# The gate product of a gated three-branch mixer by seven block products

## The chip, the cores and the metric

One core of a Trainium2 chip runs the whole kernel in one launch. The metric is device time in microseconds. TensorE (PE) multiplies matrices, VectorE (DVE) and ScalarE (ACT) do elementwise work, GpSimd (POOL) does some more of it, and SyncE (SP) issues the transfers between DRAM and the on-chip memory SBUF. PE writes its results to PSUM banks.

## What is computed

Two layers over 1024 tokens of width 1024 in float32. The change lies in the first, a mixer with three branches (a: spatial gating, b: dilated window attention, m: attention over a memory of 256 rows). Cut to what matters:

```python
h = rms_norm(x, norm_w)
proj = h @ w_in
a_u, a_v, a_z, b_q, b_k, b_v, b_z, m_q, m_z, g = jnp.split(proj, split_at, axis=-1)
...
y_m = y_m * jax.nn.silu(m_z)
gates = jax.nn.sigmoid(g.reshape(bn, s, 3, D_MODEL) + gate_b)
merged = (gates[:, :, 0] * (y_a @ proj_a)
          + gates[:, :, 1] * (y_b @ proj_b)
          + gates[:, :, 2] * (y_m @ proj_m))
x = x + merged @ w_out
```

The gate product g is 1024 tokens by 1024 by 3072 columns, and with 12 column-block pairs of 256 it is the largest product of the layer. The second layer (state-space mixer, two attentions, a final norm) is not touched by the change.

## The kernel before

Every float32 product is made of three products of a reduced-precision format: each operand is split into a high and a low part (hTh, hTl for the activations, whi, wlo for weights), and high x high, high x low and low x high are summed in PSUM. ACT makes the high part by a copy, DVE the low part by a subtraction (hilo, L266). In unitB (L372) the weights of 128 columns stand still and 512 tokens move past them: three matmuls of 128x512 for each of eight blocks k of 128 rows. In unitA the activations stand still.

The order of all instructions on each engine is fixed when the program is built. Every step is a small generator task with a priority. A planner (Sched, L81) keeps a clock for each engine from a table of costs (Eng, L145) and always continues the task that could start first. The numbers in its table are only used for the order. Pools limit how far it runs ahead: 20 tiles t4 of 128x1024 and 8 more for split weights, six t2 of 128x512, four PSUM banks "mm", three raw weight tiles, four slots "whl" for split weights (L189). Weights arrive in the order in which plan (L486) lists them: w_dma (L285) loads 512 KB into a raw tile wraw, and w_conv (L305) splits it into whi and wlo. All loads go through SP's queue.

dense (L631) sets the order of the first layer. dense_b runs the three groups of branch b in the order 1, 2, 0. For group 2 the columns (tokens) of hTh and hTl stand in residue order, four classes of tokens one after another. Ahead of group 0, reorder (L698) brings each k back to natural order, with a copy to a tile cv and a cast by DVE back into hTh[:, k] and hTl[:, k], 16 casts of 128x1024 in all, while PE does the product kv of the memory (dense_kv, L1334). dense_m (L1304) does branch m: for each head the product mz (48 matmuls), whose z_evac makes the factor silu(m_z), and then mq and the attention. dense_bz and dense_a follow, with preps in between, which prepares the second layer's constants (its transposes of ssm_c among them).

merge (L1230) then runs once for each branch in the order 0 (a), 2 (m), 1 (b). For each of the eight blocks db of 128 columns, it does the gate product for both token halves, tanh by ACT out of PSUM into tg, the projection (proj_a, proj_m or proj_b, 6, 4 or 2 blocks k) for both halves, and on DVE (tanh + 1) * projection from PSUM, added to the tile acc. The results of branches m and b wait in DRAM, and reload (L1209) brings them back and splits them. loads_1 (L1718) splits the sum for the output projection, out_proj_1 (L1754).

Of the kernel before, what the change touches and what calls it, by code (L numbers as in the profile page):

```python
# [180 lines left out]
class Kern:  # L181
# [103 lines left out]
    def w_dma(self):  # L285
        i = 0
        for w in self.wq:
            for g in w.grans:
# [16 lines left out]
    def w_conv(self):  # L305
        for w in self.wq:
            for g in w.grans:
# [11 lines left out]
                yield  # L319

# [51 lines left out]
    def unitB(self, w, csl, xh, xl, tsl, deps, cont, prio):  # L372
# [16 lines left out]
        self.s.spawn(cont(ps), prio, cont.__name__)  # L389

# [94 lines left out]

    def plan(self):  # L486
# [8 lines left out]
        for g in (1, 2, 0):  # L495
            if g == 0:
                for c in range(4):
                    add(("kv", c), I["m_w_kv"], 8, c * 256, 256)
            add(("bv", g), wi, 8, OFF_BV + g * 256, 256)
            add(("bk", g), wi, 8, OFF_BK + g * 256, 256)  # L500
            add(("bq", g), wi, 8, OFF_BQ + g * 256, 256)
        for hp in range(2):
            for s in range(2):
                add(("mz", 2 * hp + s), wi, 8, OFF_MZ + (2 * hp + s) * P, P)
            add(("mq", hp), wi, 8, OFF_MQ + hp * 256, 256)
# [125 lines left out]
    def dense(self, upto):  # L631
# [5 lines left out]
        if upto >= 2:  # L637
# [17 lines left out]
    def dense_b(self):  # L655
# [42 lines left out]
    def reorder(self, k, ev):  # L698

        for src in (self.hTh[:, k], self.hTl[:, k]):  # L700
# [225 lines left out]
    def z_evac(self, dst, ev):  # L926
        def cont(ps):
            self.A.activation(dst, ps, AF.Tanh, scale=0.5)
# [133 lines left out]
    def dense_a(self):  # L1062
# [44 lines left out]
        self.ya_ev = Ev()  # L1107
        left2 = [12]
        for j in range(6):
            um = {}  # L1110
# [28 lines left out]
            for th in range(2):  # L1139
                def cont(ps, th=th, um=um, yh=yh, yl=yl, um_ev=um_ev):  # L1140
# [12 lines left out]
                    self.rel("t2")  # L1153
                    left2[0] -= 1
                    if left2[0] == 0:
                        self.rel("t4", 2)
                        self.ya_ev.t = s.cur.t
# [34 lines left out]


# [36 lines left out]
    def merge(self, gi, yh, yl, deps):  # L1230

        s = self.s
        hh, hl = self.hk()
        first, last = self.acc is None, gi == 1
        if first:
            self.acc = {}
            self.acc_ev = [[Ev(), Ev()] for _ in range(8)]
        for db in range(8):
            wg, wp = self.w[("g", gi, db)], self.w[("p", gi, db)]
            if first and db % 2 == 0:  # L1240
                yield from self.acq("t4", 2)
                for th in range(2):
                    self.acc[db // 2, th] = self.t4(F32, "acc").rearrange("p (k t) -> p k t", k=2)
            tt = {}
            gev = [Ev(), Ev()]
            for th in range(2):
                def cont(ps, th=th, db=db, tt=tt, gev=gev):
                    if self.gb_ev.t is None:
                        yield self.gb_ev
                    yield from self.acq("t2")  # L1250
                    tt[th] = self.t2(F32, "tg")
                    self.A.activation(tt[th], ps, AF.Tanh, scale=0.5, bias=self.gb[:, gi * 8 + db:gi * 8 + db + 1])
                    self.rel("mm")
                    gev[th].t = s.cur.t
                yield from self.unitB(wg, slice(0, P), hh, hl, slice(th * 512, (th + 1) * 512), [], cont, 17)
            wg.done()
            for th in range(2):
                tsl = slice(th * 512, (th + 1) * 512)

                def cont(ps, th=th, db=db, tt=tt, gev=gev, tsl=tsl):  # L1260
                    yield gev[th]
                    a = self.acc[db // 2, th][:, db % 2, :]
                    t = tt[th]
                    if first:
                        self.V.scalar_tensor_tensor(a, t, 1.0, ps, op0=OP.add, op1=OP.mult)
                        self.rel("mm")
                    else:
                        self.V.scalar_tensor_tensor(t, t, 1.0, ps, op0=OP.add, op1=OP.mult)
                        self.rel("mm")
                        yield  # L1270
                        self.V.tensor_add(a, a, t)
                    self.rel("t2")
                    if last:
                        self.acc_ev[db][th].t = s.cur.t
                yield from self.unitB(wp, slice(0, P), lambda k: yh[k], lambda k: yl[k], tsl, deps, cont, 16)
            wp.done()
        self.rel("t4", 2 * len(yh))

# [25 lines left out]
    def dense_m(self):  # L1304
# [5 lines left out]
        self.ymT, self.mz_ev = {}, {}  # L1310
# [1515 lines left out]
```

## Time and profile before

| | us |
|---|---|
| median of 3 runs | 1783.63 (1781.91 to 1783.87) |
| profiled execution | 1782.18 |
| its span | 1780.5 |
| PE busy | 1728.5 |
| DVE busy | 1004.0 |
| ACT busy | 698.8 |
| POOL busy | 149.9 |

The span runs from the first to the last recorded instruction; the execution's own time is 1.7 us longer. Busy time is the time in which an engine has at least one instruction in flight. The matmuls of PE overlap, so the length of one matmul is more than the distance to the next. The rows name instructions as out<-in by the program's names, with partitions x elements; L239 is the helper that issues all products and L252 the transposes, L156 the helper for the other engines.

### The profile page before, as it was taken

Reading aid. Unit: us, or ns where it says so; the run is one execution under the profiler, and the core shown is the slowest. Engines: PE = TensorE matmul, PEld = TensorE weight load, DVE = VectorE, ACT = ScalarE, POOL = GpSimd, SP = SyncE. Lnnn points to the kernel's source line nnn. Section 1 sums busy time; section 2 is a strip of 40 time slices with the busy share of each in tenths; the row PEclk is TensorE's granted clock in tenths of the full one; section 3 lists DMA queues with packets and bytes.
Section 4 is the critical chain, followed back from the end, with each engine's and each line's share of the span. In section 5 each row is a group of like instructions: output and inputs, shape, how many; then the busy total and the mean of one; then the engine's idle time right before and its main releaser. Section 6 shows DMA issues by size and latency. Waiting matters only on the chain.

```text
span 1780.5 us, 26765 instructions
## 1 busy us (share of the span) xinstructions
PE 1728.5 (97%) x10215; PEld 1514.0 (85%) x10215; DVE 1004.0 (56%) x2621; ACT 698.8 (39%) x1602; POOL 149.9 (8%) x207
## 2 busy tenths in 40 slices
PE   7999979999999899999999999999999999999998
PEld 6999979998989787878888888888888788888787
DVE  6666774756655876631132243455268665655765
ACT  5464753544424122211121122366334534545632
POOL 1322322300100000000000000002000010100000
PEclk9999979999999999999999999999999999999999
DMA  6222131112033123631131122254231021112531
GB/s 223 81 67 70 49 110 36 37 51 69 28 117 84 56 78 102 206 114 54 36 101 42 52 96 66 83 179 133 66 92 47 31 72 48 37 36 83 190 127 75
DMA packets 158115, 147.80 MB, mean 83 GB/s; under 512 B 18284, under 2 KB 135582, under 8 KB 157988
## 3 DMA queue, kind: packets, MB, share of 16 engines
q1 hardware_dynamic: 157988, 146.09, 26.5%
q8 instruction: 81, 1.33, 0.3%
q14 instruction: 46, 0.38, 0.1%
HBM read 124.62 MB, written 23.80 MB: 83 GB/s over the span
## 4 chain that ended last, share of the span: by engine, by line
PE 83%; DVE 9%; ACT 3%; DMA 3%; issue 1%; POOL 1%; SPq 0%; POOLq 0%; ACTq 0%; DVEq 0%
PE psmm L239 69%; PE psx L239 9%; PE psx L252 4%; DVE dp L156 2%; ACT dp L156 1%; DVE wlo L156 1%; DVE scan L156 1%; DVE sp L156 1%; DMA sp<-in_ssm_log_step_dram 1%; DVE hTl L156 1%; DVE dst L156 0%; DMA xt<-in_x_dram 0%; SPq L256 0%; DVE St L156 0%; ACT whi L156 0%
## 5 line engine op out<-in xcount | busy, mean ns | idle before, releaser
L156 DVE TENSOR_TENSOR wlo<-wraw,whi 128x1024 fp32r<-128x1024 f32 (+3 forms) x161 | 183.0, 1139 | 212.2 <-ACT whi L156 199.4
L239 PE MATMUL psmm<-hTh,whi 128*128 128x512 f32 x672 | 266.3, 396 | 0.0
L239 PE MATMUL psmm<-whi,hTh 128*128 128x256 f32 x896 | 262.3, 293 | 1.4 <-ACT hTh L156 1.4
L239 PE MATMUL psmm<-hTl,whi 128*128 128x512 f32 x672 | 262.4, 390 | 0.0
L239 PE MATMUL psmm<-hTh,wlo 128*128 128x512 f32 x672 | 262.4, 390 | 0.0
L239 PE MATMUL psmm<-whi,hTl 128*128 128x256 f32 x896 | 254.3, 284 | 0.0
L239 PE MATMUL psmm<-wlo,hTh 128*128 128x256 f32 x896 | 254.0, 284 | 0.0
L239 PEld LDWEIGHTS psmm<-whi,hTh 128*128 128x128 f32 x896 | 173.0, 193 | 2.5 <-ACT hTh L156 1.8
L239 PEld LDWEIGHTS psmm<-wlo,hTh 128*128 128x128 f32 x896 | 173.3, 193 | 0.2
L239 PEld LDWEIGHTS psmm<-whi,hTl 128*128 128x128 f32 x896 | 172.9, 193 | 0.3 <-DVE hTl L156 0.2
L156 ACT ACTIVATE whi<-wraw 128x1024 fp32r<-128x1024 f32 (+3 forms) x161 | 158.3, 989 | 34.7 <-PE psmm L239 16.2
L239 PEld LDWEIGHTS psmm<-hTh,wlo 128*128 128x128 f32 x672 | 126.4, 188 | 27.2
L239 PEld LDWEIGHTS psmm<-hTh,whi 128*128 128x128 f32 x672 | 126.7, 189 | 26.6 <-issue 1.6
L239 PEld LDWEIGHTS psmm<-hTl,whi 128*128 128x128 f32 x672 | 126.6, 188 | 24.8
L239 PE MATMUL psmm<-h2Th,whi 128*128 128x512 f32 x352 | 143.5, 408 | 0.0
L156 ACT ACTIVATE tg<-psmm,gb 128x512 f32<-128x512 f32 x48 | 33.1, 689 | 279.0 <-PE psmm L239 242.1
L239 PE MATMUL psmm<-h2Th,wlo 128*128 128x512 f32 x352 | 137.7, 391 | 0.0
L239 PE MATMUL psmm<-h2Tl,whi 128*128 128x512 f32 x352 | 137.6, 391 | 0.0
L156 POOL TENSOR_TENSOR hst<-hst,mhalf 128x4 f32<-128x4 f32 (+1 forms) x68 | 78.3, 1153 | 260.9 <-DVE hst L156 260.9
L239 PEld LDWEIGHTS psmm<-h2Th,wlo 128*128 128x128 f32 x352 | 66.1, 188 | 14.5
L239 PEld LDWEIGHTS psmm<-h2Th,whi 128*128 128x128 f32 x352 | 66.4, 189 | 11.1
L239 PEld LDWEIGHTS psmm<-h2Tl,whi 128*128 128x128 f32 x352 | 66.4, 189 | 10.5
(354 smaller groups left out, 3373.7 us busy)
## 6 DMA issues: line engine op xcount, KB each, us to landing
wraw<-in_w_in_dram SPq DMA_DIRECT2D x96, 512.0 KB
wraw<-in_w_out_dram SPq DMA_DIRECT2D x32, 512.0 KB
ada<-in_ada_w_dram SPq DMA_DIRECT2D x24, 512.0 KB
wraw<-in_m_w_kv_dram SPq DMA_DIRECT2D x8, 512.0 KB
x2t<-in_x_dram SPq DMA_DIRECT2D x8, 512.0 KB
x_d<-x2t SPq DMA_DIRECT2D x8, 512.0 KB
xt<-in_x_dram SPq DMA_DIRECT2D x7, 512.0 KB
og_d<-rows SPq DMA_DIRECT2D x24, 132.0 KB
```

Source lines behind the costliest of these rows:

```text
L156: r = real(*a, **k)
L239: self.nc.tensor.matmul(out, lhsT, rhs, start=start, stop=stop)
L252: self.nc.tensor.transpose(out, in_, self.ident[:k, :k])
```

## The change

The gate product is no longer made block by block. project does the three projections first, moves each 128x512 result out of PSUM by ACT and writes it to DRAM (pd_d, 48 pieces of 256 KB). Meanwhile sums builds, for each of four k, sums of activation blocks: with the token halves and the k halves as a 2x2 arrangement h11, h12, h21, h22, they are T1, T3, T4 and T2, the last written over h12. gates then runs twelve rounds, four pairs of column blocks with branches 0, 2, 1 each. A round multiplies seven combinations of weight blocks by seven of activation blocks (Strassen's way, in Winograd's form), 7 x 4 x 3 = 84 matmuls where 96 stood, and joins the seven results by additions. GpSimd makes the sums of weight blocks, in four additions of 128x512 a round (pair_conv). Each round reads its projections from DRAM; the sum of the first three pairs goes to DRAM and comes back in loads_1.

Three more edits: mz of heads 0 and 1 (NZ = 2) is done ahead of the reorder, in residue order, with a strided write into ymT, and the reorder of k starts when that of k - 2 has ended; the tiles for kv are taken one at a time; and the transposes of ssm_c are placed 4 us later by the planner. In loads_1 the four loads of x follow the first split.

```diff
+    def pair_conv(self, w):
...
+        yield from split(0, r0)
...
+        r1, ws = w.raw[1], w.raw[2]
+        G = self.G
+        G.tensor_add(ws[:, lo], r1[:, lo], r1[:, up])
+        G.tensor_sub(ws[:, up], ws[:, lo], r0[:, lo])
+        G.tensor_sub(r1[:, lo], r0[:, lo], r1[:, lo])
+        G.tensor_sub(r0[:, up], r0[:, up], ws[:, up])
+        yield
+        yield from split(2, ws)
+        self.rel("raw")
+        yield from split(1, r1)
+        self.rel("raw")
+        yield from split(3, r0[:, up], 512)
+        self.rel("raw")
...
+    NZ = 2
...
             if g == 0:
+                for h in range(self.NZ):
+                    add(("mz", h), wi, 8, OFF_MZ + h * P, P)
...
         for i, name, nk in ((0, "proj_a", 6), (2, "proj_m", 4), (1, "proj_b", 2)):
             for db in range(8):
-                add(("g", i, db), wi, 8, OFF_G + i * D + db * P, P)
                 add(("p", i, db), I[name], nk, db * P, P)
+        for dbp in range(4):
+            for i in (0, 2, 1):
+                w = self.w["g", i, dbp] = WP(wi, OFF_G + i * D + 2 * dbp * P)
+                self.wq.append(w)
...
-            self.acc = None
-            yield from self.merge(0, self.yaH, self.yaL, [self.ya_ev] * 6)
         if upto >= 3:
-            yield from self.merge(2, *self.reload(self.ym_d, self.ym_ev))
-            r = self.reload(self.yb_d, self.yb_ev)
-            self.loads_1()
-            yield from self.merge(1, *r)
...
+            ym = self.reload(self.ym_d, self.ym_ev)
+            yield from self.project(0, self.yaH, self.yaL, self.ya_ev)
+            for k in range(3):
+                s.spawn(self.sums(k, ym[2]), 22, "sums")
+            yb = []
+            s.spawn(self.reload_b(yb, ym[2]), 11, "reload_b")
+            yield from self.project(2, *ym)
...
+            yield from self.project(1, *yb)
+            yield from self.gates()
...
             if g == 0:
+                self.ymT, self.mz_ev = {}, {}
+                for h in range(self.NZ):
+                    yield from self.dense_mz(h, True)
+                order = []
                 for k in range(8):
-                    s.spawn(self.reorder(k, conv_ev[k]), 15, "reorder")
+                    order.append(s.spawn(self.reorder(k, conv_ev[k], order[k - 2:k - 1]), 15, "reorder"))
                 yield from self.dense_kv()
...
+    def project(self, gi, yh, yl, deps):
...
+                self.A.activation(t, ps, AF.Copy)
+                self.rel("mm")
+                yield
+                self.dma(self.pd_d[gi][db, :, tsl], t, 256)
...
+    def sums(self, k, before):
...
+        V.tensor_sub(f, h12, h11)
+        V.tensor_add(f, f, l12)
+        V.tensor_sub(f, f, l11)
+        yield from self.hilo(T1[:, lo], T1[:, up], f)
...
+    def gates(self):
...
+                A.activation(t, t, AF.Tanh, scale=0.5, bias=self.gb[:, gi * 8 + 2 * dbp + q:gi * 8 + 2 * dbp + q + 1])
+                yield pl_ev[n]
+                a = self.acc[dbp, th][:, q]
+                if first:
+                    V.scalar_tensor_tensor(a, t, 1.0, a, op0=OP.add, op1=OP.mult)
+                else:
+                    V.scalar_tensor_tensor(t, t, 1.0, pl[n][th][:, q], op0=OP.add, op1=OP.mult)
+                    yield
+                    V.tensor_add(a, a, t)
...
+            def keep(x, ps, c=c, ev=ev):
+                yield from self.acq("t2")
+                c[x] = self.t2(F32, "c" + x)
+                A.activation(c[x], ps, AF.Copy)
+                self.rel("mm")
+                ev[x].t = s.cur.t
...
+            def sum_u(x, ps, c=c, ev=ev, gate=gate):
...
+                V.tensor_add(c["U"], ps, c["P1"])
...
+                V.tensor_add(c["P5"], c["P5"], c["U"])
...
+                V.tensor_add(c["U"], c["U"], c["P7"])
...
+                V.tensor_add(c["P7"], c["P7"], c["P5"])
...
+                yield from gate(c["P7"], 1, 1)
...
+                V.tensor_add(c[x], ps, c[x])
...
+            for i, off, r, f, args, last_use in ((0, 0, "11", keep, ("P1",), 0), (2, 0, "T1", keep, ("P5",), 0),
+                                                 (1, 0, "T3", keep, ("P7",), 0), (2, 512, "T2", sum_u, ("U",), 1),
+                                                 (0, 512, "21", add, ("P1", 0, 0, ("U",)), 1),
+                                                 (3, 0, "22", add, ("P5", 0, 1, ("X", "C")), 1),
+                                                 (1, 512, "T4", add, ("U", 1, 0, ("Y",)), 1)):
...
+                if last_use:
+                    self.rel("whl")
...
+                self.s.cur.t += 4
```

The first place is DVE's queue at the first cast of the reorder. Q and qn belong to the queries of branch b's attention, hst to the norms, rows to its results, cv to the reorder. Before:

```order
L156 TENSOR_TENSOR Q_2676<-psx_2671,Q_2676 64x2x128
L156 CAST Q_2676<-Q_2676 64x2x128
L156 TENSOR_TENSOR wlo_2690<-wraw_1940,whi_2689 128x1024
L156 CAST hTh<-cv_2692 128x1024
L156 CAST hTh<-cv_2694 128x1024
L156 TENSOR_REDUCE hst_2697<-qn_2696 128x4
L156 TENSOR_SCALAR hst_2697<-hst_2697 128x4
```

Now:

```order
L156 SCALAR_TENSOR_TENSOR ymT_2863<-ymT_2863,psmm_2864 128x2x256
L156 COPY rows_2972<-psx_3016 128x128
L156 COPY rows_2972<-psx_3030 128x128
L156 TENSOR_TENSOR wlo_3052<-wraw_2789,whi_3051 128x1024
L156 CAST hTh<-cv_3058 128x1024
L156 CAST hTh<-cv_3060 128x1024
L156 TENSOR_REDUCE hst_3094<-qn_3093 128x2
L156 TENSOR_SCALAR hst_3094<-hst_3094 128x2
L156 SCALAR_TENSOR_TENSOR ymT_2863<-ymT_2863,psmm_2995 128x2x256
L156 CAST hTl<-cv_3105 128x1024
```

The casts have moved behind the last queries and results of group 2's attention and stand among the evacuations of mz (ymT).

The second place is DVE's queue in the middle of the gate product, where tg is a tanh and acc the sum of the branches. Before:

```order
L156 SCALAR_TENSOR_TENSOR tg_9318<-tg_9318,psmm_9352 128x512
L156 TENSOR_TENSOR acc_8356<-acc_8356,tg_9318 128x512
L156 SCALAR_TENSOR_TENSOR tg_9359<-tg_9359,psmm_9373 128x512
L156 TENSOR_TENSOR wlo_9393<-wraw_9233,whi_9392 128x512
L156 TENSOR_TENSOR acc_8357<-acc_8357,tg_9359 128x512
L156 TENSOR_TENSOR wlo_9453<-wraw_9292,whi_9452 128x1024
```

Now, with cP and cU the kept products and their sums, and pl a projection from DRAM:

```order
L156 SCALAR_TENSOR_TENSOR cU_10718<-cU_10718,pl_10521 128x512
L156 TENSOR_TENSOR wlo_10804<-wraw_10635,whi_10803 128x512
L156 TENSOR_TENSOR acc_10241<-acc_10241,cU_10718 128x512
L156 TENSOR_TENSOR cU_10869<-psmm_10847,cP_1560_10809 128x512
L156 TENSOR_TENSOR wlo_10867<-wraw_10783,whi_10866 128x1024
L156 TENSOR_TENSOR cP_1563_10827<-cP_1563_10827,cU_10869 128x512
L156 TENSOR_TENSOR cU_10869<-cU_10869,cP_1567_10851 128x512
L156 TENSOR_TENSOR cP_1567_10851<-cP_1567_10851,cP_1563_10827 128x512
```

GpSimd's queue at that place, where nothing stood, has the sums of raw weights:

```order
L156 TENSOR_TENSOR wraw_10383<-wraw_10363 128x512
L156 TENSOR_TENSOR wraw_10383<-wraw_10383,wraw_10340 128x512
L156 TENSOR_TENSOR wraw_10363<-wraw_10340,wraw_10363 128x512
L156 TENSOR_TENSOR wraw_10340<-wraw_10340,wraw_10383 128x512
L156 TENSOR_TENSOR wraw_10514<-wraw_10503 128x512
```

The projection no longer comes from PSUM, the additions of the kept products have come in between the splits of weights, and the splits wlo now follow GpSimd's sums.

## Rows read from the trace of the kernel before

**Rows 1.** The page's totals: busy time by engine; the chain that ended last

```profile
span 1780.5 us, 26765 instructions
...
PE 1728.5 (97%) x10215; PEld 1514.0 (85%) x10215; DVE 1004.0 (56%) x2621; ACT 698.8 (39%) x1602; POOL 149.9 (8%) x207
...
PE 83%; DVE 9%; ACT 3%; DMA 3%; issue 1%; POOL 1%; SPq 0%; POOLq 0%; ACTq 0%; DVEq 0%
```

**Rows 2.** Busy time by stretch; instructions in brackets, granted clock, DMA share, GB/s

```profile
core 0: us, PE busy (x) PEld busy (x) DVE busy (x) ACT busy (x) POOL busy (x), PEclk, DMA share, GB/s
210.00:250.00 40.00, 27.32 (x164) 25.16 (x162) 37.18 (x84) 26.99 (x51) 18.38 (x11) 0.74 0.24 73
250.00:260.00 10.00, 10.00 (x88) 9.97 (x87) 5.98 (x22) 8.61 (x31) 0.00 (x0) 1.00 0.50 145
340.00:420.00 80.00, 80.00 (x574) 74.50 (x574) 50.87 (x160) 41.55 (x122) 9.19 (x16) 1.00 0.14 39
780.00:1130.00 350.00, 350.00 (x1542) 288.86 (x1541) 99.63 (x136) 71.14 (x104) 0.00 (x0) 1.00 0.20 63
1130.00:1240.00 110.00, 109.03 (x512) 90.47 (x511) 59.98 (x88) 60.33 (x114) 10.08 (x14) 1.00 0.47 150
1180.00:1190.00 10.00, 10.00 (x54) 8.54 (x53) 5.59 (x11) 6.56 (x15) 1.10 (x2) 1.00 0.94 309
```

**Rows 3.** PE groups of 740 to 1135 us: count, busy us, mean ns, idle

```profile
L239 PE MATMUL psmm<-hTh,whi 128*128 128x512 f32 x384 | 149.4, 389 | 0.0
```

**Rows 4.** DVE groups of 745 to 1140 us, shapes kept apart

```profile
L156 DVE TENSOR_TENSOR wlo<-wraw,whi 128x1024 fp32r<-128x1024 f32 x26 | 31.8, 1224 | 115.7 <-ACT whi L156 107.3 <-issue 8.4
L156 DVE TENSOR_TENSOR acc<-acc,tg 128x512 f32<-128x512 f32 x32 | 22.0, 687 | 0.4
L156 DVE SCALAR_TENSOR_TENSOR tg<-tg,psmm 128x512 f32<-128x512 f32 x32 | 22.0, 686 | 72.9 <-PE psmm L239 72.9
...
L156 DVE TENSOR_TENSOR wlo<-wraw,whi 128x512 fp32r<-128x512 f32 x8 | 5.5, 683 | 0.0
```

**Rows 5.** ACT groups of the same stretch

```profile
L156 ACT ACTIVATE tg<-psmm,gb 128x512 f32<-128x512 f32 x48 | 33.1, 689 | 279.0 <-PE psmm L239 242.1 <-issue 36.8
L156 ACT ACTIVATE whi<-wraw 128x1024 fp32r<-128x1024 f32 x26 | 27.4, 1052 | 9.4 <-PE psmm L239 9.4
...
L156 ACT ACTIVATE whi<-wraw 128x512 fp32r<-128x512 f32 x8 | 5.0, 623 | 3.1 <-PE psmm L239 3.1
```

**Rows 6.** GpSimd groups of the whole execution

```profile
L156 POOL TENSOR_TENSOR hst<-hst,mhalf 128x2 f32<-128x2 f32 x20 | 26.2, 1309 | 115.6 <-DVE hst L156 115.6
...
L156 POOL CAST Q<-Q 64x256 fp32r<-64x256 f32 x48 | 19.3, 402 | 69.2 <-ACT Q L156 53.9 <-issue 13.7 <-POOL hst L156 0.7
...
L156 POOL MEMSET WoZ<- 128x512 f32 x4 | 2.1, 527 | 7.0 <-DVE h2Tl L156 7.0
```

**Rows 7.** Timeline of GpSimd, then of DVE, from 226 us: start, length

```profile
226.22 6.96 POOL L156 TENSOR_TENSOR hst<-hst,mhalf 128x2 f32<-128x2 f32 x1 [0.57 <-DVE hst L156]
...
226.04 2.30 DVE L156 CAST hTl<-cv 128x1024 fp32r<-128x1024 f32 x2
228.19 1.29 DVE L156 TENSOR_TENSOR wlo<-wraw,whi 128x1024 fp32r<-128x1024 f32 x1
```

**Rows 8.** Timeline of PE in the reorder, with the idle time before each

```profile
220.07 0.58 PE L239 MATMUL psmm<-wlo,memh 128*128 128x256 f32 x1 [3.05 <-DVE wlo L156]
...
224.47 0.69 PE L252 MATMUL psx<-ident,qn 128*128 128x128 f32 x2 [1.68 <-DVE mk L156]
...
229.53 0.58 PE L239 MATMUL psmm<-wlo,memh 128*128 128x256 f32 x1 [4.16 <-DVE wlo L156]
...
238.53 0.44 PE L252 MATMUL psx<-ident,qn 128*128 128x128 f32 x2 [1.61 <-DVE Q L156]
```

**Rows 9.** DVE groups of 210 to 250 us

```profile
L156 DVE CAST hTl<-cv 128x1024 fp32r<-128x1024 f32 x8 | 10.0, 1290 | 0.0
```

**Rows 10.** Timeline of PE at the state-space layer's preparation

```profile
592.57 0.45 PE L252 MATMUL psx<-ident,sp 128*128 128x128 f32 x1 [4.57 <-DMA sp<-in_ssm_c_re_dram]
```

More of the change, by code (lines that the diff above doesn't have):

```diff
@@ L306, in w_conv @@
         for w in self.wq:
+            if isinstance(w, WP):
+                yield from self.pair_conv(w)
+                continue
             for g in w.grans:
@@ L696, in dense_b, with reorder @@
                 w.done()
-    def reorder(self, k, ev):
+    def reorder(self, k, ev, before):
+        for e in before:
+            yield e
         for src in (self.hTh[:, k], self.hTl[:, k]):
@@ L1106, in dense_a @@
         self.vn_ev = [Ev() for _ in range(6)]
-        self.ya_ev = Ev()
+        self.ya_ev = [Ev() for _ in range(6)]
         left2 = [12]
         for j in range(6):
+            leftj = [2]
             um = {}
@@ L1191, in a_mix, with reload_b, unit, cont @@
         self.rel("x")
+    def reload_b(self, out, before):
+        for e in before:
+            yield e
+        out.extend(self.reload(self.yb_d, self.yb_ev))
+        self.s.spawn(self.sums(3, out[2]), 22, "sums")
+    def project(self, gi, yh, yl, deps):
+        s = self.s
+        def unit(db, th, left):
+            tsl = slice(th * 512, (th + 1) * 512)
+            def cont(ps):
+                yield from self.acq("t2")
+                t = self.t2(F32, "pj")
+                self.A.activation(t, ps, AF.Copy)
+                self.rel("mm")
+                yield
+                self.dma(self.pd_d[gi][db, :, tsl], t, 256)
+                self.rel("t2")
+                left[0] -= 1
+                if left[0] == 0:
+                    self.pd_ev[gi][db].t = s.cur.t
+            return self.w["p", gi, db], lambda k: yh[k], lambda k: yl[k], tsl, cont, deps
+        for d0 in range(0, 8, 2):
+            ls = [[2], [2]]
+            us = [unit(d0 + j, th, ls[j]) for j in range(2) for th in range(2)]
+            yield from self.unitsB(us, [len(yh) - 1] if d0 == 0 else [], 16) if d0 == 0 else self.each_b(us)
+            for j in range(2):
+                self.w["p", gi, d0 + j].done()
+        self.rel("t4", 2 * len(yh))
@@ L1228, in reload @@
         return yh, yl, done
[L1230 to L1277, printed above, removed]
     def mem_norm(self):
@@ L1346, in cont @@
                 def cont(ps, cb=cb, b=b, ev=ev):
+                    while len(self.mkv) < (2 if cb < 2 else 4):
+                        yield lambda: len(self.mkv) >= (2 if cb < 2 else 4)
                     if cb < 2:
@@ L1364, in dense_kv, with kv_alloc @@
         self.rel("t4", 4)
+    def kv_alloc(self):
+        for i in range(4):
+            yield from self.acq("t4")
+            t = self.t4(F32R, "mk" if i < 2 else "mv")
+            self.mkv.append(t.rearrange("p (h m) -> p h m", h=4) if i < 2 else t.rearrange("p (b v) -> p b v", b=2))
+        self.mkh, self.mkl, self.mvh, self.mvl = self.mkv
     def pt_alloc(self, st):
@@ L2753, with __init__ @@
     __slots__ = ("k0", "nk", "raw", "hi", "lo", "arrived", "ready")
+class WP:
+    def __init__(self, src, c0):
+        self.src, self.c0 = src, c0
+        self.raw, self.arrived, self.ready = [], [Ev() for _ in range(3)], [Ev() for _ in range(4)]
+        self.hi, self.lo = [None] * 4, [None] * 4
 class W:
```

243 lines of the change are left out of this document (220 added, 23 removed).

## The prediction

> **What bounds the kernel now.** I read the page first: busy time by engine and the chain of work that ended last. PE is busy 97% of the 1780.5 us and carries 83% of the chain, DVE 9% [rows 1]. The mean hides where PE is not the limit, so the second view is the busy time by stretch. In the merge, from 780 to 1130 us, PE is busy for all 350.00 us at a granted clock of 1.00, while DVE works 99.6 us, ACT 71.1 and GpSimd nothing [rows 2]. What ends last there is the next matmul, and the stretch costs its number of matmuls times their pitch: 350.00 / 1542 = 0.2270 us. The groups give 389 ns for one [rows 3], which is no price, since these pipelined matmuls overlap. The gate product is three rows of 384, 1152 matmuls or 261.5 us. One other stretch matters. From 210 to 250 us, where the columns of hTh and hTl are put back into natural order, PE is busy 27.32 of 40 us at a mean clock of 0.74 and does 164 matmuls; DVE is busy 37.18. The next 10 us hold 88 matmuls with PE full [rows 2]; at that pace, 0.1136 us, the 164 would have taken 18.6. So some 21 us are lost there, and DVE is what PE waits for.
>
> **The seven products.** Twelve rounds (four pairs of column blocks, three branches) do 84 matmuls of 128x512 where 96 stood. That is 144 fewer, each 0.2270 us in a stretch where nothing else ends last: **-32.7 us**. The operands keep partition count, columns and number format, so I keep the pitch. A round is now 84 x 0.2270 = 19.07 us of PE, and this is the cover for all that the round adds elsewhere.
>
> **The rounds' other engines.** DVE in a round of branch 2 or 1: four adds from PSUM, three among kept products, four scalar_tensor_tensor and four accumulations, 15 in all at 0.687 (the nearest rows, 686 and 687 ns), three splits of 1024 columns at 1.224 and one of 512 at 0.683 [rows 4]: 14.65 us. ACT: three copies out of PSUM and four tanh at up to 0.689, three splits at 1.052 and one at 0.623 [rows 5]: 8.6 us. Both fit in 19.07. GpSimd has four additions of 128x512, and no row of before shows one. From below, a memset of that size took 0.527 us; from above, the small power operation's 1.309 us as a fixed part with the cast's columns on top (0.402 us for 256, so 0.80 for 512) make 2.1 us [rows 6]. I take 0.80, the cast's price by columns, since an add of equal dtype is nearest to it: 3.2 us a round. Even with DVE standing still for all of it a round is 17.9 us, under 19.07.
>
> What speaks against this is how DVE and GpSimd get on. At 226.22 us one of those 1.309 us power operations took 6.96, while DVE ran casts and splits with no gap beside it [rows 7]. In a round DVE has 4.4 us free, so a GpSimd operation gets in, but late. Who waits for that: ACT's split of the sums is queued behind GpSimd, and behind this on ACT stand the copies that free the PSUM banks. The cover: a slot for split weights comes free after the fourth, fifth, sixth and seventh product of a round, and what is put in it is first read by the next round's first, second, third and sixth, so for three of four 36 matmuls, 8.2 us, lie between; a split takes 1.05 + 1.22 = 2.3 of them, 5.9 are left for the queues. I charge **+2 us** for the twelve rounds, from 0 to 12 (1 us a round).
>
> [...]
>
> **Into and out of the rounds.** The projections keep their 576 matmuls. Their 48 copies out of PSUM (0.689 at most) lie on ACT under 131 us of PE: nothing. The sums of activation blocks are 14 DVE operations for each of four k, 4 x 14 x 0.687 = 38.5 us, under proj_m (192 matmuls, 43.6 us) and proj_b (96, 21.8). Two k must go under proj_b: 19.2 us, with four splits of yb, at 0.687 as well, and the first gate weights behind them, about 25 against 21.8; the first product, which needs no sum, covers 2.7. I charge 1 us for the first projection's entry, 2 between projections (the last tile of ym is loaded only once proj_a's tiles are released), 2 at the first round, and 3 at the end, where tanh, product, accumulation and splits of the last round's blocks must be done before the output projection has used up its first 36 matmuls: **+8 us**, from 0 (all covered) to 16 (each twice as long). The detour over DRAM is 12.6 MB out and in and 3.1 MB of acc out and in, 31 MB in some 360 us: 87 GB/s on top of 63, about what 1130 to 1240 us moved (150 GB/s at a share of 0.47), with 309 seen at 0.94 [rows 2]. Nothing, while loads stay a round ahead. SP issues 108 more transfers; the weight loads are queued behind writes that wait for ACT's copies, with three raw buffers for cover.
>
> **The two mz products, moved.** 96 matmuls, 21.8 us of PE, now stand ahead of the reorder, and the reorder goes two k at a time. PE's waits there end on DVE: 3.05, 1.68, 4.16 and 1.61 us [rows 8]. The reorder's 16 casts at 1.29 us [rows 9] are 20.6 us and still must come after the last product that reads the old order; with the rest of DVE's 37.18 busy us, 36 us of DVE stand against kv's 192 matmuls of 256 columns, 192 x 0.1136 = 21.8. What the mz products buy is a DVE that has worked off its earlier queue, and about 5 us of casts begun under the last unit. So 36 - 21.8 - 5 = 9 to 11 us stay lost of 21: **-10 us**. Were PE covered but for a few waits it would be -18; did the casts just begin later, with the same lack of cover, -3.
>
> They are missing as cover in the attention over memory. There PE was full for 80 us while DVE worked 50.87 and ACT 41.55 [rows 2]; 21.8 us less PE work raises DVE to some 51 of 58. **+2 us**, 0 to 6. The transposes of ssm_c waited 4.57 us for a DMA [rows 10]; they are placed later, behind others that wait for a chain of DVE that ends at about the same time: **-1 us**, -5 to 0.
>
> **Sum.** Against the profiled execution, 1782.18 us (1.7 beyond its span; 1.45 under the median of 1783.63): -32.7 + 2 + 8 - 10 + 2 - 1 = -31.7, so 1750.5, and by the median **1752**.
>
> **Rivals.** *DVE and GpSimd lengthen the rounds.* With 1.6 us for an addition and strict turns, a round is 14.65 + 6.4 = 21.05, 2.0 over PE's; twelve make +24 in place of +2: 1774, or 1763 if half the turns overlap. For it: the 6.96 us. [...] *The mz products win back the whole stretch*: -21.4 in place of -10, 1741. For it: the four waits named all end on DVE. Against: the casts cannot start before the reads end. *Slower:* GpSimd's additions at their upper bound, 2.1 us, with DVE standing still meanwhile, so that a round is 14.65 + 8.4 = 23.05, +47.8 over twelve in place of +2: 1798. All other terms together gain 33.7, or 2.8 a round, so this turns to a loss from 21.9 us a round, 1.8 us per addition. Against: no row supports that an add pays the power operation's price. That the change does not shorten PE's work can be left out: the instruction order has exactly 144 fewer.
>
> **How the numbers follow.** Forecast 0.70, the longer rounds 0.17, the whole stretch won back 0.07, slower 0.04, and 0.02 for a time near the old one by several small losses. A measurement can tell about 0.2%, 3.6 us, from no change. Faster by more: 0.93, with 0.01 of the longer rounds ending in between; within: 0.03; slower: 0.04. The range's low end takes -18 for mz and +2 for the entries (1738); its high end -3 for mz and +12 for the rounds (1769, and I write 1770). Between lie most of the forecast, the won-back stretch and the milder half of the longer rounds.
>
> **What would show it.** Right: PE full through the twelve rounds at 19.0 to 19.3 us each, DVE near 14.7 in each, GpSimd additions under 1.2 us; PE waits of about 10 us in the reorder; the matmul groups 144 shorter. Wrong: PE waits in each round that end on ACT's whi or GpSimd's sums, additions of 1.8 us or more, PE at the lower clock level in the rounds, or a first or last round with a wait over 5 us.

## The result and the profile after

The changed kernel takes 1753.26 us (median of 6 runs, 1749.88 to 1755.69), the kernel before 1783.28 beside it. The ratio is 0.9831, with a 95% interval from 0.9817 to 0.9845. The forecast was 1752 us, in a range from 1738 to 1770. The page's totals of the profiled execution:

```profile
span 1751.6 us, 27160 instructions
...
PE 1699.8 (97%) x10071; PEld 1485.7 (85%) x10071; DVE 1139.0 (65%) x2785; ACT 772.2 (44%) x1726; POOL 219.3 (13%) x255
```

Against [rows 1], PE has exactly 144 records and 28.7 us of busy time less, and the span is 28.9 us shorter. DVE has 135 us more, ACT 73, GpSimd 69. The span has followed PE's busy time.

Busy time by stretch, with the columns of [rows 2]: rounds two to twelve, and the stretch in which PE waits at the first projection.

```profile
892.00:1098.00 206.00, 206.00 (x911) 170.52 (x910) 160.65 (x195) 86.95 (x125) 60.96 (x40) 1.00 0.40 131
...
748.00:752.00 4.00, 2.12 (x12) 1.69 (x10) 1.51 (x2) 0.00 (x0) 0.00 (x0) 0.86 0.97 288
752.00:756.00 4.00, 4.00 (x15) 3.52 (x15) 1.00 (x3) 0.00 (x0) 0.00 (x0) 0.50 0.87 302
```

In the rounds PE is never idle, and 911 matmuls in 206 us are 0.226 us each, the pitch of [rows 2] (350.00 / 1542 = 0.227). DVE works 160.65 / 206 x 19.05 = 14.9 us a round, where 14.65 was forecast for branches 2 and 1. PE's waits from 726 to 1200 us, in all, times, longest:

```profile
PE psmm L239 <- ACT whi L156: 2.5, 3, 1.3
PE psx L239 <- DVE macc L156: 2.4, 2, 1.9
PE psmm L239 <- DVE mgl L156: 2.3, 2, 1.9
PE psmm L239 <- DVE wlo L156: 0.7, 2, 0.5
PE psmm L239 <- ACT mgh L156: 0.4, 1, 0.4
```

Here macc is the running sum that reduces the weights of the second layer's modulation (ada), mgh and mgl are the split sum that the output projection reads. None of the waits lies inside the steady rounds: they stand at the first projection (macc), at proj_b and in the first round (whi, wlo) and at the output projection's entry (mgl, mgh). The kernel before has no wait in the same stages. By starts of single matmuls in the timelines, of the kernel before and then of the changed one, the gain is divided like this (us from the span's start; a stage ends where the next begins):

```profile
739.81 0.39 PE L239 MATMUL psmm<-hTh,whi 128*128 128x512 f32 x1
...
1135.70 0.39 PE L239 MATMUL psmm<-whi,mgh 128*128 128x512 f32 x1
...
1228.21 0.39 PE L239 MATMUL psmm<-h2Th,whi 128*128 128x512 f32 x1
```

```profile
726.56 0.48 PE L239 MATMUL psmm<-yah,whi 128*128 128x512 f32 x1
...
1100.83 0.39 PE L239 MATMUL psmm<-whi,mgh 128*128 128x512 f32 x1
...
1198.97 0.39 PE L239 MATMUL psmm<-h2Th,whi 128*128 128x512 f32 x1
```

| | before | after | change |
|---|---|---|---|
| first matmul of the merge, or of the projections | 739.81 | 726.56 | -13.25 |
| projections and gates, to the first matmul of the output projection | 395.89 | 374.27 | -21.62 |
| output projection, to the first of the next layer's products | 92.51 | 98.14 | +5.63 |
| from there to the last matmul | 544.58 | 544.67 | +0.09 |

The middle stage before was 1728 matmuls, 392.3 us at 0.227, and 3.6 us of losses; after, 1584 are 359.6 us, with 14.7 of losses. So the 144 matmuls gave their 32.7 us, and 11.1 came back inside the stage: 6.5 at the first projection, 2.3 at proj_b, 2.4 in the first round.

### The profile page after: what moved, and what is told of

It is laid out like the page before. It is cut to its first block, busy times and chain, and to the rows that moved or that the text cites. A ratio compares the mean times of both kernels' runs of the same rounds, so it can differ in the third digit from the quotient of the medians.

```text
span 1751.6 us, 27160 instructions
## 1 busy us (share of the span) xinstructions
PE 1699.8 (97%) x10071; PEld 1485.7 (85%) x10071; DVE 1139.0 (65%) x2785; ACT 772.2 (44%) x1726; POOL 219.3 (13%) x255
## 4 chain that ended last, share of the span: by engine, by line
PE 39%; DVE 7%; ACT 2%; issue 1%; DMA 1%; POOL 0%; POOLq 0%; SPq 0%; ACTq 0%; DVEq 0%
PE psmm L239 33%; PE psx L239 4%; DVE dp L156 2%; PE psx L252 2%; ACT dp L156 1%; DVE wlo L156 1%; DVE scan L156 1%; DVE dst L156 1%; DVE St L156 0%; DVE cP L156 0%; DVE zs L156 0%; ACT whi L156 0%; DVE dO L156 0%; DMA macc<-acc_d 0%; POOL dst L156 0%
## 5 line engine op out<-in xcount | busy, mean ns | idle before, releaser
L156 DVE TENSOR_TENSOR wlo<-wraw,whi 128x1024 fp32r<-128x1024 f32 (+3 forms) x185 | 211.8, 1148 | 117.2 <-ACT whi L156 116.3
L239 PE MATMUL psmm<-hTh,whi 128*128 128x512 f32 x480 | 192.2, 401 | 0.0
L156 ACT ACTIVATE whi<-wraw 128x1024 fp32r<-128x1024 f32 (+3 forms) x185 | 177.6, 968 | 23.5 <-DMA wraw<-in_w_out_dram 9.0
L239 PE MATMUL psmm<-hTh,wlo 128*128 128x512 f32 x480 | 187.6, 391 | 0.2 <-DVE wlo L156 0.2
L239 PE MATMUL psmm<-hTl,whi 128*128 128x512 f32 x480 | 187.5, 391 | 0.0
L239 PEld LDWEIGHTS psmm<-hTh,wlo 128*128 128x128 f32 x480 | 90.3, 188 | 20.0 <-DVE wlo L156 0.6
L239 PEld LDWEIGHTS psmm<-hTh,whi 128*128 128x128 f32 x480 | 90.5, 188 | 19.1 <-issue 1.8
L239 PEld LDWEIGHTS psmm<-hTl,whi 128*128 128x128 f32 x480 | 90.6, 189 | 16.9
L156 POOL TENSOR_TENSOR hst<-hst,mhalf 128x4 f32<-128x4 f32 (+1 forms) x68 | 73.1, 1077 | 249.8 <-DVE hst L156 249.8
L239 PE MATMUL psmm<-T,whi 128*128 128x512 f32 x288 | 88.8, 389 | 1.0 <-ACT whi L156 1.0
L239 PEld LDWEIGHTS psmm<-h2Th,whi 128*128 128x128 f32 x352 | 66.4, 189 | 11.1
```

The lines of the kernel that those rows point to most:

```text
L156: r = real(*a, **k)
L239: self.nc.tensor.matmul(out, lhsT, rhs, start=start, stop=stop)
```

## The experiments

Each kernel was timed beside runs of the kernel before. A change to one place lets the planner set the order of all later steps anew, so I read the stage in the trace beside every median.

**mz_only: the edits ahead of the merge, put into the kernel before.**

```diff
             if g == 0:
+                for h in range(self.NZ):
+                    yield from self.dense_mz(h, True)
...
+                    order.append(s.spawn(self.reorder(k, conv_ev[k], order[k - 2:k - 1]), 15, "reorder"))
...
+                self.s.cur.t += 4
```

> The kernel before with only the edits ahead of the merge (two mz products ahead of the reorder, reorder two at a time, kv tiles one at a time, ssm_c transposes 4 us later); the merge stays as it was. Theory A, from the two traces: the stretch up to the first matmul of the merge is 15 us shorter (726.6 against 741.5 us), and this stays: 1783 - 15 = 1768. Theory B, from the prediction's terms (-10 + 2 - 1): 1774. Rival: the merge cannot use it, since the modulation's weights (ada, 24 loads of 512 KB in two buffers) end no earlier, and PE waits for them: 1772 to 1776 with a wait before an ones x macc matmul.

Measured: 1768.4 us, ratio 0.9918 (0.9897 to 0.9939). The gain is 14.7 us, as theory A has it. The merge begins at 726.81 us, as early as the changed kernel's projections, and lasts 395.89 us, as before. So 14.7 of the change's 30 us have nothing to do with the gate product. The rival's wait for macc does not appear: the second reduction ones x macc starts at 743.13 us without one.

**nz0: the changed kernel without early mz products.**

```diff
-    NZ = 2
+    NZ = 0
```

> The changed kernel with no mz product ahead of the reorder (NZ = 0); all the rest stays, the reorder two k at a time too. Theory A: the two mz products carry the 12.7 us that the reorder stretch gained: 1753 + 12 = 1765, and PE's waits in the reorder are back (about 10 us of idle time, low clock after them). Rival: the gain came from the reorder going two k at a time and from kv's tiles, so that the time stays within 3 us of 1753. Prediction's terms (+10 - 2): 1761.

Measured: 1759.28 us (ratio 0.986, 0.9843 to 0.9877), 6.0 above the changed kernel. This is half of what theory A said, and more than the rival's 3: more than one edit shares the gain.

**reo_only: in the kernel before, only the reorder two k at a time.**

```diff
-                    s.spawn(self.reorder(k, conv_ev[k]), 15, "reorder")
+                    order.append(s.spawn(self.reorder(k, conv_ev[k], order[k - 2:k - 1]), 15, "reorder"))
```

> The kernel before with only the reorder two k at a time. The changed kernel without early mz products kept about 6 us of the gain ahead of the merge. Theory: the chained reorder does that, since DVE then takes kv's splits between the casts, earlier than it did: 1783 - 6 = 1777. Rival: the single allocation of kv's tiles does it, and this kernel stays at 1783, within 2 us.

Measured: 1776.79 us, ratio 0.9967 (0.9955 to 0.998), 5.9 us faster than before. The stretch from 210 to 250 us of this kernel, as in [rows 2]:

```profile
210.00:250.00 40.00, 33.40 (x238) 30.69 (x236) 36.66 (x98) 30.65 (x68) 9.73 (x11) 0.87 0.34 102
```

PE is busy for 33.4 us there and does 238 matmuls, against 27.32 and 164 before. DVE is as full as before; what changed is what it does first. Before, the 16 casts of all eight k ran from 207 to 235 us with little between them. Now two k at a time are in work, the casts reach to 256 us, and the steps that PE waits for come between them:

```order
L156 COPY rows_2570<-psx_2786 128x128
L156 TENSOR_TENSOR wlo_2771<-wraw_2244,whi_2770 128x1024
L156 TENSOR_TENSOR Q_2812<-psx_2714,Q_2812 64x2x128
L156 CAST Q_2812<-Q_2812 64x2x128
```

Before, a cast of hTl stood two places behind this split of wlo. This edit's 5.9 us and the 6.0 of nz0 make 11.9 of the 14.7 of mz_only; the remaining 2.8 were not divided further, and the rival that kv's tiles, taken one at a time, give some of them was not run alone.

**no_delay: the changed kernel without the later transposes of ssm_c.**

```diff
-                self.s.cur.t += 4
```

> The changed kernel without the 4 us by which the planner places the transposes of ssm_c later. Theory, the prediction's term: the wait of 4.6 us for the load of ssm_c comes back at 580 to 590 us and the wait of 2.7 us for av goes, 1 to 2 us more: 1754.5. Rival: the wait is not hidden by anything else, and the whole of it is lost: 1758.

Measured: 1753.89 us (ratio 0.9844, 0.9829 to 0.9858), 0.6 above the changed kernel, which these runs can't tell from nothing. PE's timeline, first without the delay, then with it:

```profile
580.41 0.30 PE L252 MATMUL psx<-ident,sp 128*128 128x128 f32 x1 [4.23 <-DMA sp<-in_ssm_c_re_dram]
...
582.32 2.93 PE L239 MATMUL psx<-aw,av 128*128 128x128 f32 x16 [2.69 <-DVE av L156]
```

One wait stands in for the other, as the prediction's term had it (4.57 us in [rows 10]); the waits there are 4.2 us without the delay and 2.7 with it.

**plain8: the changed kernel with eight plain products per round.** The projections still come first and go through DRAM; the sums of activations and of weights are left out.

```diff
-            for i, off, r, f, args, last_use in ((0, 0, "11", keep, ("P1",), 0), ...
+            for q in range(2):
+                for th in range(2):
+                    yield from self.acq("mm")
+                    ps = self.ps("mm")
+                    for k in range(8):
...
+                    s.spawn(direct(ps, q, th), 16, "direct")
```

> The changed kernel with eight plain products per round in place of seven: projections first and through DRAM as now, no sums of activation blocks, no sums of weight blocks, tanh straight from PSUM, 144 matmuls more. Theory A: the seven products are worth their 32.7 us less the waits that their sums cause at proj_b and in the first round (2.3 + 2.4 us in the trace): 1753 + 32.7 - 5 = 1781. Rival 1: all 32.7 and no more: 1786. Rival 2: DVE, ACT and GpSimd lengthen the rounds by 1 us or more each, which the trace would then have hidden in its busy PE: 1753 + 32.7 - 12 or more, 1774 or less.

Measured: 1772.94 us, ratio 0.9943 (0.9922 to 0.9964), 19.7 above the changed kernel. The rounds of this kernel:

```profile
868.00:1128.00 260.00, 260.00 (x1149) 215.29 (x1148) 88.86 (x112) 61.48 (x82) 0.00 (x0) 1.00 0.40 134
```

PE is full here too, at 0.226 us a matmul. To the first matmul of the output projection the two kernels differ by 1128.96 - 1100.83 = 28.1 us, what theory A says (32.7 - 4.7). From there plain8 needs 92.5 us, like the kernel before, and the changed kernel 98.1. So the seven products give 32.7 and lose 2.3 at proj_b, 2.4 in the first round and 5.6 at the exit: 22.4 by the trace, 19.7 by the medians. What I left out of the expectation was the exit. The measured time is one that rival 2 allowed (1774 or less), but its reason is not there: from the first matmul of the gates to that of the output projection plain8 needs 30.0 us more, the 32.7 less the first round's loss, so the changed kernel's rounds hide no lengthening. Against mz_only (1768.4), plain8 shows what the detour costs by itself: projections first and through DRAM, 4.5 us by the medians, whose intervals overlap, and 401.05 - 395.89 = 5.2 by the traces. It lies at the first projection, where PE waits 1.4 us for macc and then runs at the lower clock:

```profile
752.00:756.00 4.00, 4.00 (x16) 3.71 (x17) 1.00 (x3) 0.00 (x0) 0.00 (x0) 0.50 1.03 360
```

**gp_double: twice the work on GpSimd.** The first two of a round's four additions are done three times over.

```diff
+        for _ in range(2):
+            G.tensor_add(ws[:, lo], r1[:, lo], r1[:, up])
+            G.tensor_sub(ws[:, up], ws[:, lo], r0[:, lo])
```

> The changed kernel with eight additions on GpSimd per round in place of four (the first two of the four are done three times over; the result is the same). Theory A, from the trace of the changed kernel: the four additions take 6.5 us per round and stand in a ring (raw weights loaded after the last split of the round before, GpSimd, splits) that has only about 2 us to spare between GpSimd's end and the split that follows it; 6.5 us more make each round 4 to 5 us longer, with PE waiting for whi or wlo of the T products: 1753 + 12 x 4.5 = about 1805. Rival 1, by the prediction's 5.9 us of slack per slot: GpSimd is idle for 12 us of each round, so up to 1 us a round, 1765 at most. Rival 2, strict turns with DVE: 14.7 + 13 = 27.7 us a round, 1855.

Measured: 1812.46 us in a single run, 59 us above the changed kernel and 30 above the one before. PE's waits from 860 to 1160 us, the beginnings of two rounds on GpSimd, and the rounds as a whole with the columns of [rows 2]:

```profile
PE psmm L239 <- DVE wlo L156: 23.9, 12, 3.8
PE psmm L239 <- ACT whi L156: 18.0, 9, 6.4
...
936.17 1.28 POOL L156 TENSOR_TENSOR wraw<-wraw 128x512 f32<-128x512 f32 x1 [8.72 <-DMA wraw<-in_w_in_dram]
...
960.20 1.29 POOL L156 TENSOR_TENSOR wraw<-wraw 128x512 f32<-128x512 f32 x1 [11.29 <-DMA wraw<-in_w_in_dram]
...
868.00:1164.00 296.00, 254.21 (x1013) 201.80 (x1012) 208.15 (x212) 99.67 (x141) 152.32 (x96) 0.92 0.34 110
```

This round takes 960.20 - 936.17 = 24.0 us, 5.0 more. By the trace all twelve take 64 us more (295.2 against 231.1), and some 5 us came back at other places. GpSimd is still idle for some 11 us of a round, waiting for raw weights, so this is no lack of GpSimd time. It stands in a ring. In the changed kernel, GpSimd's three later additions, then a tanh and the first split of the sums on ACT, the split's other half on DVE, and PE's first use of it:

```profile
940.56 5.22 POOL L156 TENSOR_TENSOR wraw<-wraw,wraw 128x512 f32<-128x512 f32 x3
...
947.09 0.72 ACT L156 ACTIVATE cP<-cP,gb 128x512 f32<-128x512 f32 x1 [7.72 <-DVE cP L156]
947.72 1.05 ACT L156 ACTIVATE whi<-wraw 128x1024 fp32r<-128x1024 f32 x1
...
949.06 1.22 DVE L156 TENSOR_TENSOR wlo<-wraw,whi 128x1024 fp32r<-128x1024 f32 x1
...
951.23 0.62 PE L239 MATMUL psmm<-T,whi 128*128 128x512 f32 x2
```

GpSimd ends at 945.8, ACT begins 1.9 us later, since a tanh that waits for DVE's additions stands ahead in its queue, the split is done at 950.3, and PE reads it at 951.2: about 1 us to spare at the end and 1.9 in front. The 6.5 us added less these two make 3.6, and PE's waits, 41.9 us, are 3.5 a round. The rest of the 5.0 goes with PE's clock: 0.92 in the mean over these rounds, against 1.00 in the changed kernel's. That DVE's slowed additions and splits lengthen the ring too was not taken apart.

**dve_sums: the sums of weight blocks on DVE.**

```diff
-        G = self.G
+        G = self.V
```

> The changed kernel with the four sums of weight blocks on DVE in place of GpSimd. In the trace the two engines slow each other: cU<-cU,cP takes 1581 ns where such an add alone takes 687, GpSimd's additions 1.3 to 2.3 us. Theory: PE is full in the rounds either way, DVE has 14.7 + 4 x 0.69 = 17.4 us of 19.05, so the time stays at 1753, within 3 us, DVE's adds all take 0.69 us and the first round's waits get 1 to 2 us shorter. Rival: with 1.6 us of DVE left free per round, splits and results come late: PE waits in the rounds, 1760 or more.

Measured: 1744.28 us, ratio 0.9783 (0.9768 to 0.9798), 9 us faster than the changed kernel, outside what either theory allowed. Groups of the changed kernel, GpSimd's of the whole execution, then DVE's of 874 to 1100 us:

```profile
L156 POOL TENSOR_TENSOR wraw<-wraw,wraw 128x512 f32<-128x512 f32 x36 | 57.7, 1625 | 6.2 <-DVE wlo L156 5.3
...
L156 POOL TENSOR_TENSOR wraw<-wraw 128x512 f32<-128x512 f32 x12 | 16.7, 1389 | 312.1 <-DMA pd_d<-pj 184.9 <-DMA wraw<-in_w_in_dram 127.2
```

```profile
L156 DVE TENSOR_TENSOR cU<-cU,cP 128x512 f32<-128x512 f32 x12 | 19.0, 1581 | 0.4
...
L156 DVE TENSOR_TENSOR cU<-psmm,cP 128x512 f32<-128x512 f32 x12 | 8.3, 691 | 40.4 <-PE psmm L239 40.4
```

And of dve_sums, from 920 to 1000 us:

```profile
L156 DVE TENSOR_TENSOR wraw<-wraw,wraw 128x512 f32<-128x512 f32 x13 | 8.3, 688 | 0.2
...
L156 DVE TENSOR_TENSOR cU<-psmm,cP 128x512 f32<-128x512 f32 x5 | 3.5, 692 | 18.8 <-PE psmm L239 18.8
...
L156 DVE TENSOR_TENSOR cU<-cU,cP 128x512 f32<-128x512 f32 x4 | 2.7, 684 | 0.0
```

The same addition on DVE takes 684 ns where GpSimd is silent and 1581 where it works beside; one with an operand in PSUM takes 691 and 692. An addition of weights costs 688 ns here and 1389 or 1625 on GpSimd. In the window from 920 to 1000 us DVE is busy for 63.6 us in this kernel and for 63.4 in the changed one: taking over GpSimd's work cost DVE nothing. The sums are 11.7 us of it; about as much, 10.7 us, had gone into 13 splits at 1401 ns in place of 1215 and eight additions of kept products at 1776 and 1664 in place of 685.

Yet the steady rounds gained nothing by it, since PE was full in them either way. Where the 9 us come from (7.0 between the two profiled executions): the way from the first matmul of the gates to that of the output projection is 1.1 us shorter, all in the first round, and the output projection's stage 5.2 (92.95 against 98.14). The first projection is 2.5 us shorter and begins 2.8 us later, but both stand ahead of the first sum of weights, so these and what is left of the 9 us are not shown to be the edit's. In the first projection PE waited 1.5 us for macc, and unlike in plain8 its clock stayed up:

```profile
752.00:756.00 4.00, 3.17 (x22) 2.96 (x23) 1.77 (x4) 0.00 (x0) 0.00 (x0) 1.00 1.06 360
```

The 5.2 are an effect of order. The queue of transfers at the exit, of the changed kernel and then of dve_sums (macc names here the tile into which a spilled sum is loaded back):

```profile
1083.01 5.67 SPq L256 DMA_DIRECT2D wraw<-in_w_out_dram  x3
1088.73 0.46 SPq L256 DMA_DIRECT2D macc<-acc_d  x1
1096.46 0.37 SPq L256 DMA_DIRECT2D wraw<-in_w_out_dram  x1
1096.93 0.41 SPq L256 DMA_DIRECT2D macc<-acc_d  x1
```

```profile
1081.25 3.92 SPq L256 DMA_DIRECT2D wraw<-in_w_out_dram  x2
1085.21 0.47 SPq L256 DMA_DIRECT2D macc<-acc_d  x1
1087.79 0.37 SPq L256 DMA_DIRECT2D wraw<-in_w_out_dram  x1
1088.20 0.47 SPq L256 DMA_DIRECT2D macc<-acc_d  x1
```

In the changed kernel the last spilled sum stands behind a fourth weight load, which needs one of three raw tiles and so the first split of w_out. In dve_sums it stands behind the third, and is issued 8.7 us earlier. PE then has no wait for mgl.

**out_wide: the output projection begins with four units.**

```diff
-            yield from self.unitsA([unit(0, bb) for bb in range(2)], [6], 20)
-            yield from self.unitsA([unit(0, bb) for bb in (2, 3)], [2, 4, 6], 20, True)
+            if th == 0:
+                yield from self.unitsA([unit(0, bb) for bb in range(4)], [4, 6], 20, True)
+            else:
...
```

> The changed kernel with the output projection's first half started on four units over four blocks k each (48 matmuls) in place of two units over six. Theory: PE's waits at 1104 to 1108 us for the split of the acc that comes back from DRAM (0.6, 0.7 and 1.9 us) and the lower clock level for 5 us behind them are covered by 10.9 us of matmuls: 5 us less, 1748. Rival: four units need four PSUM banks while the last round's products still hold some, so that the wait moves to the banks: within 2 us of 1753.

Measured: 1747.64 us, ratio 0.9801 (0.9787 to 0.9816), 5.6 less than the changed kernel, as the theory said. The stage of the output projection falls from 98.1 to 93.2 us, 4.9 of it. This settles the exit: waits of 2.7 us in all for mgl and mgh, and the lower clock behind them (0.50 from 1110 to 1112 us in the changed kernel, matmuls 0.43 us apart).

**best_b: dve_sums and out_wide together.**

> The sums of weight blocks on DVE and the output projection started on four units. Theory: both alone took away the same wait at the output projection's entry (98.1 us from its first matmul to the next layer's became 92.9 and 93.2), so that together they give no more than one: 1744, within 2 us. Rival, if the gains add: 1744 - 5.6 = 1739.

Measured: 1744.87 us (ratio 0.979, 0.9776 to 0.9805), the same as dve_sums. Both removed one and the same wait, so their gains don't add.

**mod_late: the modulation's reduction 8 us later.** In the changed kernel PE stands in the first projection ahead of the products ones x macc. PE's timeline there:

```profile
750.48 3.26 PE L239 MATMUL psx<-ones,macc 128*128 128x1 f32 x16 [1.89 <-DVE macc L156]
...
754.17 0.63 PE L239 MATMUL psmm<-yal,whi 128*128 128x512 f32 x1
754.60 0.63 PE L239 MATMUL psmm<-yah,wlo 128*128 128x512 f32 x1
```

Matmuls then stand 0.43 us apart for 4 us, at half the granted clock. From 748.3 to 760 us 7.2 us go to other than the projection's matmuls at their pitch; the sixteen small products took 1.7 of them before as well (750.70 to 752.40 us), so a wait of 1.9 us cost 5.5. In mz_only, where PE is as early, this reduction found its load in place; what holds the load up here stands in the new order, with projections first, as plain8's wait at the same place says too.

```diff
             if part < 2:
+                self.s.cur.t += 8
+                yield
                 yield from self.acq("x")
```

> The changed kernel with the small matmuls that reduce the modulation's weights (ones x macc, at 748 to 753 us in the trace) placed 8 us later by the planner. Theory: PE waited there 1.9 us for a DVE step that waited for a load of ada, and ran at the lower clock level for some 5 us behind it, 6 to 7 us in all; later they find macc ready: 1753 - 6 = 1747. Rival: the loads of ada, slowed by the projections' traffic, end later still, and the same wait stands at the new place: 1753, within 2 us.

Measured: 1756.37 us, ratio 0.984 (0.9819 to 0.9861): no gain. The wait for macc went from 2.4 to 0.5 us and the first projection ended 4 us earlier, but then PE and the queue of transfers showed this:

```profile
802.88 0.80 PE L239 MATMUL psmm<-yh,whi 128*128 128x512 f32 x1 [4.03 <-ACT yh L156]
...
794.57 0.23 SPq L256 DMA_DIRECT2D modt<-in_ada_b_dram  x1
798.00 0.21 SPq L256 DMA_DIRECT2D mod_d<-modt  x1
798.31 0.82 SPq L256 DMA_DIRECT2D yr<-ym_d  x2
```

A reload of ym, issued at 787.05 in the changed kernel, now stands behind the modulation's last write, which waits for PE at its later place. The wait moved to proj_m: 7.5 us more there, and 2.9 more at the exit. Of the rival I had only this half right: the loads of ada were not the cause.

**best_a: dve_sums, and the reduction 3 us later.**

```diff
             if part < 2:
+                self.s.cur.t += 3
```

> The changed kernel with the sums of weight blocks on DVE and the two ones x macc reductions placed 3 us later. With the sums on DVE, PE still waits 3.1 us for macc at 751 to 778 us and runs at the lower clock level behind the first. Theory: 3 us are enough for the wait of 1.6 us and too little to delay the reload of ym, which an 8 us delay did: 1744 - 4 = 1740. Rival: the loads of ada fill the time between, and the wait moves on as it did with 8 us: 1744, within 2 us.

Measured: 1741.34 us, ratio 0.977 (0.9754 to 0.9786), the fastest version. It stands 2.9 us under dve_sums, which lies inside the intervals of the two. The trace supports a part of it: PE has no wait for macc left, and the first projection is 1.6 us shorter than in dve_sums. The lower clock that the expectation saw behind that wait was not there: in dve_sums the granted clock is 1.00 from 748 to 760 us.

```profile
757.24 1.84 PE L239 MATMUL psx<-ones,macc 128*128 128x1 f32 x16
```

**best_c: dve_sums, and a third buffer for ada.**

```diff
-        yield from self.acq("t4", 4)
+        yield from self.acq("t4", 5)
...
-        ch = [self.t4(F32, "ada") for _ in range(2)]
+        ch = [self.t4(F32, "ada") for _ in range(3)]
```

> The sums of weight blocks on DVE and three buffers for the loads of ada in place of two. Theory: the reduction waits for a load that is issued only when one of two buffers is free; with a third it is issued a step earlier, and PE's 3.1 us of waits for macc and the lower clock behind them go: 1744 - 5 = 1739. Rival: the transfers themselves are the limit there (233 to 317 GB/s, a DMA share of 0.76 to 0.92), so that a third buffer gives nothing: 1744, within 2 us.

Measured: 1743.66 us (ratio 0.9784, 0.977 to 0.9799), no more than dve_sums. The waits for macc fell from 3.1 to 0.9 us, yet the time did not follow. The first stretch of this kernel:

```profile
726.00:748.00 22.00, 21.29 (x96) 17.44 (x95) 16.17 (x19) 4.31 (x8) 0.00 (x0) 0.92 0.80 268
```

The first projection is only 0.7 us shorter than in dve_sums: behind a wait of 0.7 us the mean clock of this stretch is 0.92, where dve_sums kept 1.00 behind a wait of 1.5. The time is the rival's, but that the transfers are the limit is not shown: with the third buffer DVE did 19 instructions from 726 to 748 us, against 16 in dve_sums, so its loads did come sooner.

## Why the prediction held, and where its steps did not

That the sum came out 1 us from the median is luck: two misses stood against each other. It gave too little ahead of the merge (13.3 us by the trace in place of 9) and too little loss at the entries (16.8 in place of 8).

**The seven products**, -32.7: right, in size and reason. The pitch held with sums as operands (0.226 us against 0.227), and PE was full.

**The rounds' other engines**, +2 from 0 to 12: the steady rounds cost nothing. But the step's working failed twice. A GpSimd addition was taken at 0.80 us and takes 1.39 to 1.63 us in the mean (1.27 at the least), the price of the first rival; one of the four takes 2.3, more than the 1.8 that was to be a sign of being wrong. That rival did not come true since not all of DVE's instructions were slowed: beside GpSimd an addition with both operands in SBUF took 1581 ns in the mean against 684 without it, one with an operand in PSUM 691 against 692. A round holds 14.9 us of DVE and 5.6 of GpSimd, 20.5 in all, in 19.05. That 14.9 came near the forecast 14.65 is luck too. By dve_sums I estimate DVE's own work at (63.6 - 11.7) / 80 x 19.05 = 12.4 us a round, the shorter rounds of branch 0 among them. The forecast added whole lengths, where each operation starts some 0.08 us before the last has ended, and had nothing for the slowing, some 2.5 us. And the 5.9 us of slack were wrong: I counted from the release of a slot for split weights, while GpSimd's sums are done only some 3 us before the split would come late. By these 3 us the rival on the slower side, 8.4 us a round on GpSimd, would still have been covered, an estimate; at the 13 us of gp_double the kernel is at 1812.

**Into and out of the rounds**, +8: 6.5 at the first projection in place of 1, 2.3 at proj_b and none at proj_m in place of 2 between, 2.4 at the first round as forecast with 2, 5.6 at the exit in place of 3, 16.8 together. This is beyond the 16 that I set as the end. The failed term is the first projection's, and the exit's is nearly twice its size. The prediction gave the entry 1 us without a reason and does not name the reduction of the modulation's weights, which stands in the same stretch of PE's queue, with a load behind it that came no earlier though PE did. Nor has it a price for the clock behind a wait, where one of 1.9 us cost 5.5.

**The two mz products, moved**, -10, with dense_m +2 and ssm_c -1: 13.3 us gained in the trace (14.7 by the medians of mz_only) in place of 9. The step that failed is that the reorder two at a time was given nothing. It alone brings 5.9 us (reo_only), the early mz products 6.0 (nz0), and 2.8 stay open. I took DVE's work as one sum of 36 us against 22 of cover; but part of PE's waits came from the order within that work. The ssm_c term, -1, came out as -0.6, within the spread. PE's waits left in the stretch from 240 to 280 us are 4.5 us long, less than the 10 foreseen.

## What to carry to other kernels

Where PE is full, matmuls taken away are worth their pitch, here 0.227 us each, and the risk lies at the edges: list what else stands in PE's queue where a stage now begins earlier, and price a wait by its length, with a margin for matmuls at a lower clock behind it (here 0.43 us apart in place of 0.227, at 0.50). When one engine is overloaded and another waits for it, look at the order of its work before adding cover: a limit of two casts in flight was worth as much as 22 us of other matmuls. Before work goes to a helper engine, find the ring it stands in and try it on the engine with the gaps: DVE did the same sums in 0.69 us each and was no longer busy than before, since its own additions and splits had been longer beside GpSimd's (1664 and 1776 ns in place of 685, 1401 in place of 1215); where PE is full this gains nothing by itself.

## What was not expected of the hardware

One engine did the work of two in the same time: from 920 to 1000 us DVE was busy for 63.4 us with GpSimd's 29.9 beside it, and for 63.6 us with those sums on top and GpSimd idle. An idle time of PE of 1.9 us was followed by some 4 us at a granted clock of 0.50 (752 to 756 us, matmuls 0.43 us apart), so that the stop cost nearly three times its length. But the length of a stop did not tell its cost: at the same place 1.4 us in plain8 and 0.7 us in best_c were followed by the lower level (0.50 from 752 to 756 us, 0.92 in the mean from 726 to 748), and 1.5 us in dve_sums by 1.00.
